# A bidirectional encoder layer on one core: the order of operand preparation in the down projection, and where the residual additions stand

## Chip, core and metric

One of the cores of a Trainium2 chip runs the whole program. The metric is the device time of one execution in microseconds; the kernel before takes 2554.81 us (median of 3 runs, 2551.83 to 2556.84). Less is better.

## What is computed

Two requests of 1024 tokens (with 16 meta tokens in front) go one after the other through the same layer in float32: attention and a gated linear recurrence side by side, an output projection, and a SwiGLU feed-forward block. The part at issue is the last:

```python
xn = rms_norm(h, norm_ffn_g[l])
g, u = jnp.split(xn @ w_gate_up[l], 2, axis=-1)   # 1024 -> 2 x 2816
h = h + (jax.nn.silu(g) * u) @ w_down[l]          # 2816 -> 1024, the down projection
...
h = rms_norm(h, final_norm_g)
```

## The kernel before

Each request is called a trunk. For each trunk the kernel runs a projection phase, attention, and `ffn`. A float32 product is made of three TensorE passes: each operand is split into a high part (a cast to the rounded type fp32r, on ACT) and a low part (the rest, a subtraction on DVE or POOL), and `mm3` adds high x high, high x low and low x high into one PSUM bank.

Both products of the feed-forward block are done with a seven-product (Strassen-like) scheme. The activations and the weight are cut into 2 x 2 blocks; sums and differences of blocks are multiplied, and each product is added into several blocks of the result. In the down projection the seven products are passes, `DN` = P1, P2, P4, P5, P7, P6, P3, in that order. A pass sums over 22 hidden tiles in `NC` = 11 **units** (index c). A unit is four `mm3`, one for each of four PSUM banks q: 12 matmuls of 128x128 by 128x512. Its operands are two tiles of the shape 2 x 512 (high and low): `sop`, made from an activation block `A[i, j, c]`, and `top`, made from rows of the down weight (`raws`, loaded to one of four buffers, or `trun`, rows kept through several passes).

What sets the order of work around the change:

- All engines run their own queue in order. The kernel writes the order itself: `ffn` goes through `units`, and at the start of unit n calls `prep(n)`, then issues the matmuls of unit n (`gu_unit` for gate and up, `dn_unit` for down).
- `prep(n)` prepares units ahead as long as operand tiles are left: `cap` = 6 of a ring of seven, a down unit takes two. So in a down pass, when unit n is issued, the operands of n and n+1 are under way and n+2 is prepared.
- `prep_dn(p, c)` is the first half: the sums and differences that the pass needs (in place, on blocks of activations or on weight rows), then the casts on ACT. P1 and P3 need no sums. P2 has one on DVE, P4 one on DVE and one that takes turns between DVE (even c) and POOL (odd c) as well as a copy on ACT, P5 two on DVE, P7 one on DVE, P6 one on DVE and two more of which one falls to DVE and one to POOL.
- `prep_dn_lo(p, c)` is the second half: the low part of `top` on DVE and that of `sop` on POOL. After it the raw buffer is free. `lows(m)` does this for all prepared units below m and then calls `load`, which issues on SP the load of the next raw tile into the buffer that came free; SP's queue waits there until the low part has read it.
- When a pass is done, its four banks are added into the residual `T.h` on DVE, one to four additions for each bank (`C[p]`). They are kept in the list `adds` and are issued within the units of the next pass, in `dn_unit`, after the matmuls of banks q = 1 and q = 3. All must be issued by the last unit, since the pass after that uses the same banks.

In the last pass of the first trunk (P3) the second trunk's inputs are loaded, normalised and transposed in between.

Of the kernel before, what the change touches and what calls it, by code (L numbers as in the profile page):

```python
# [36 lines left out]
NC = NHT // 2  # L37
# [207 lines left out]
def hymba_kernel(ctx, tc, ins, outs, dbg=None):  # L245
# [182 lines left out]
    def mm3(out, lh, ll, rh, rl, first, last, more=False):  # L428

        pe.matmul(out, lhsT=lh, rhs=rh, start=first, stop=False, skip_group_check=more)  # L430
        pe.matmul(out, lhsT=lh, rhs=rl, start=False, stop=False, skip_group_check=more)
        pe.matmul(out, lhsT=ll, rhs=rh, start=False, stop=last, skip_group_check=more)
# [1179 lines left out]
    def ffn_stream(T, b):  # L1612
# [42 lines left out]
        def load(limit=None):  # L1655

            while r_next[0] < len(items):
                i = r_next[0]
                if i >= 4 and items[i - 4][0] not in freed:
                    break  # L1660
                key, shape, parts = items[i]
                r = slot(raw_tags[i % 4], shape, name="wraw")
                for dst, src in parts:
                    sync.dma_start(out=dst(r), in_=src)
                raws[key] = r
                r_next[0] += 1
# [88 lines left out]
        def prep_dn_lo(p, c):  # L1755
            src, s, sop, top = half.pop((p, c))
            dve.tensor_tensor(top[:, 1], src, fv(top[:, 0]), ALU.subtract)
            pool.tensor_tensor(sop[:, 1], s, fv(sop[:, 0]), ALU.subtract)
            ops["dn", p, c] = (q4((sop[:, 0], sop[:, 1])), (top[:, 0], top[:, 1]))
            if p in ("P2", "P6", "P3"):  # L1760
                if c % 2 or c == NC - 1:
                    freed.add((p, c - c % 2))
            elif p in ("P4", "P5"):
                freed.add((p, c))
# [3 lines left out]
        def lows(n):  # L1768

            while n_lo[0] < min(n, T.n_prep2):  # L1770
                u = T.units[n_lo[0]]
                if u[0] == "dn":
                    prep_dn_lo(*u[1:])
                n_lo[0] += 1
            load()
# [3 lines left out]

        def prep(n):  # L1780

            lows(n + 2)
            while T.n_prep2 < len(T.units):
                u = T.units[T.n_prep2]
                need = 1 if u[0] == "gu" else 2
                out = sum(1 if x[0] == "gu" else 2 for x in T.units[n:T.n_prep2])
                if out + need > cap:
                    break
                if T.before_prep(u) is False:
                    break  # L1790
                (prep_gu if u[0] == "gu" else prep_dn)(*u[1:])
                T.n_prep2 += 1
                load()
            lows(n + 1)

        T.before_prep = lambda u: u[1:] == ("P1", 0)
        load()
        prep(0)
        T.prep_ops = prep

    def ffn(T, b, nxt):
# [9 lines left out]
        def bank(s, i, name):  # L1811
            tag = PB[s][i]
            return mk_d([P, 512], name) if tag is None else ps.tile([P, 512], F32, tag=tag, name=name)
# [113 lines left out]
        adds = []  # L1927
        banks = {}

        def add(p, q, i, l, sign, bk):  # L1930
            hs = T.h[:, 2 * q + i - 1, (l - 1) * 512:l * 512]
            dve.tensor_tensor(hs, hs, bk, ALU.add if sign > 0 else ALU.subtract)

        def dn_unit(p, c):
            n = DN.index(p)
            if c == 0:
                banks[n] = [bank(n % 2, q, "dn") for q in range(4)]
            (sh, sl), (th, tl) = ops.pop(("dn", p, c))
            for q in range(4):
                mm3(banks[n][q], sh[:, q], sl[:, q], th, tl, c == 0, c == NC - 1)  # L1940
                if q % 2 and adds:
                    adds.pop(0)()
            if c == NC - 1:
                assert not adds
                for q in range(4):
                    for i, l, sign in C[p]:
                        adds.append(lambda q=q, i=i, l=l, sign=sign, bk=banks[n][q]: (add(p, q, i, l, sign, bk), T.h_adds.add((p, q, i, l))))
# [103 lines left out]
        for n, (kind, p, i) in enumerate(units):  # L2051
            cur[0] = n
            if n == len(GU):
                for _ in side:
                    pass
            T.prep_ops(n)
            assert T.n_prep2 > n
            if kind == "gu":
                gu_unit(p, i)
                gu_hook(p, i)  # L2060
            else:
                dn_unit(p, i)
                if p == "P3" and not T.d_free and not adds:
                    T.d_free = True
                    if nxt is None:
                        gf_b = slot(S_GR, [P, D], name="gfin")
                        sync.dma_start(out=gf_b, in_=bcast_rows(ins["final_norm_g"]))
                        odd = spawn(finals(range(1, TT, 2), lambda t: True, slot("s4", [P, D], name="junk")), 3.0)
# [91 lines left out]
```

## Time and profile before

| | |
|---|---|
| median of 3 runs | 2554.81 us (2551.83 to 2556.84) |
| the profiled execution | 2563.52 us |
| its span, first to last instruction | 2561.7 us |
| mean granted TensorE clock | 0.97 |
| busy share PE / DVE / ACT / POOL | 93 / 70 / 46 / 52% |
| down projection, first trunk | 1021.95 to 1285.04 us |
| down projection, second trunk | 2298.05 to 2547.45 us |

Times in the rows are us from the span's start. PE is TensorE, with PEld its weight loads, which overlap the matmuls; DVE is VectorE, ACT ScalarE, POOL GpSimd, SP the queue that issues DMAs. `out<-in` are the program's names: `wop` an operand tile, `dn` the banks, `h` the residual, `wraw` and `trun` weight rows, and `aA`, `aB`, `aC`, `aD`, `aS`, `aV` the activation blocks. All compute instructions stand on line 118, that of a helper, so that groups are told apart by tiles.

### The profile page before, as it was taken

Reading aid. Unit: us, or ns where it says so; the run is one execution under the profiler, and the core shown is the slowest. Engines: PE = TensorE matmul, PEld = TensorE weight load, DVE = VectorE, ACT = ScalarE, POOL = GpSimd, SP = SyncE. Lnnn points to the kernel's source line nnn. Section 1 sums busy time; section 2 is a strip of 40 time slices with the busy share of each in tenths; the row PEclk is TensorE's granted clock in tenths of the full one; section 3 lists DMA queues with packets and bytes.
Section 4 is the critical chain, followed back from the end, with each engine's and each line's share of the span. In section 5 each row is a group of like instructions: output and inputs, shape, how many; then the busy total and the mean of one; then the engine's idle time right before and its main releaser. Section 6 shows DMA issues by size and latency. Waiting matters only on the chain.

```text
span 2561.7 us, 34088 instructions
## 1 busy us (share of the span) xinstructions
PE 2385.7 (93%) x12402; PEld 2002.5 (78%) x12402; DVE 1782.2 (70%) x2462; ACT 1168.3 (46%) x2083; POOL 1335.8 (52%) x1222
## 2 busy tenths in 40 slices
PE   7998999989999999998889889999799999999887
PEld 7878998867888888766677789988678888878665
DVE  6787888876555555778866778888665555557787
ACT  4456666654223232333535566666442222224434
POOL 5434766554444444445763356665544444444456
PEclk9998999989999999999999889999899999999999
DMA  5112000112222224741330130001122232247402
GB/s 137 37 35 101 19 17 18 42 66 65 76 78 82 88 74 156 271 148 38 136 128 19 35 108 18 9 18 42 66 66 74 83 91 74 83 159 276 149 30 111
DMA packets 189703, 212.77 MB, mean 83 GB/s; under 512 B 24272, under 2 KB 141008, under 8 KB 188512
## 3 DMA queue, kind: packets, MB, share of 16 engines
q1 hardware_dynamic: 189536, 210.60, 24.9%
q8 instruction: 98, 1.61, 0.3%
q14 instruction: 69, 0.57, 0.1%
HBM read 168.45 MB, written 39.85 MB: 81 GB/s over the span
## 4 chain that ended last, share of the span: by engine, by line
PE 65%; DVE 18%; ACT 6%; POOL 5%; issue 5%; DMA 1%; SPq 0%; ACTq 0%; DVEq 0%; POOLq 0%
PE gu L118 33%; PE op L118 5%; PE dn L118 5%; PE S L118 4%; PE pvo L118 4%; PE ptp L118 3%; DVE wop L118 3%; ACT wop L118 2%; PE pin L118 2%; PE qp L118 2%; DVE arena L118 2%; PE gp L118 2%; PE pg L118 1%; DVE m L118 1%; ACT arena L118 1%
## 5 line engine op out<-in xcount | busy, mean ns | idle before, releaser
L118 PE MATMUL dn<-wop 128*128 128x512 f32 x1848 | 463.4, 403 | 44.8 <-DVE wop L118 34.0
L118 PEld LDWEIGHTS dn<-wop 128*128 128x128 f32 x1848 | 340.7, 189 | 160.8 <-DVE wop L118 68.0
L118 PE MATMUL gu<-xT,wop 128*128 128x512 f32 x1408 | 371.2, 394 | 0.0
L118 POOL TENSOR_TENSOR pexp<-pexp,rsum 128x1024 f32<-128x1024 f32 x128 | 243.3, 1900 | 234.1 <-DVE rsum L118 150.7
L118 POOL TENSOR_TENSOR wop<-wraw,wop 128x512 fp32r<-128x512 f32 x176 | 230.7, 1311 | 217.0 <-ACT wop L118 217.0
L118 POOL TENSOR_TENSOR wop<-wsum,wop 128x512 fp32r<-128x512 f32 x132 | 171.7, 1301 | 269.0 <-ACT wop L118 269.0
L118 PEld LDWEIGHTS gu<-xT,wop 128*128 128x128 f32 x1408 | 264.0, 188 | 59.4
L118 PE MATMUL gu<-xB,wop 128*128 128x512 f32 x1056 | 265.5, 399 | 2.9 <-DVE xB L118 2.9
L118 ACT CAST wop<-wraw 128x512 fp32r<-128x512 f32 x264 | 162.5, 616 | 229.3 <-DVE wraw L118 159.9
L118 PE MATMUL gu<-xH,wop 128*128 128x512 f32 x1056 | 254.7, 396 | 1.7 <-DVE act L118 1.7
L118 PEld LDWEIGHTS gu<-xH,wop 128*128 128x128 f32 x1056 | 198.7, 188 | 50.5 <-issue 2.5
L118 PEld LDWEIGHTS gu<-xB,wop 128*128 128x128 f32 x1056 | 199.5, 190 | 49.0 <-DVE xB L118 3.6
L118 ACT CAST pt<-ptp 128x512 fp32r<-128x512 f32 x256 | 149.1, 586 | 127.9 <-PE ptp L118 126.7
L118 DVE TENSOR_REDUCE m<-S 128x1 f32<-128x1041 f32 x128 | 158.2, 1236 | 52.7 <-PE S L118 51.9
L118 ACT ACTIVATE pexp<-S,m 128x1041 f32<-128x1041 f32 x128 | 145.0, 1133 | 57.8 <-DVE m L118 55.1
L118 DVE TENSOR_TENSOR pt<-ptp,pt 128x512 fp32r<-128x512 f32 x256 | 168.2, 682 | 3.4 <-ACT pt L118 2.2
L118 PE MATMUL ptp<-idf,pexp 128*128 128x128 f32 x1024 | 157.0, 278 | 11.8 <-DVE pt L118 6.7
L118 PE MATMUL pvo<-pt,vst 128*128 128x256 f32 x1024 | 155.3, 295 | 3.6 <-DVE attnT L118 3.5
L118 PE MATMUL S<-kh,qs 128*128 128x348 f32 (+1 forms) x384 | 136.6, 358 | 19.3 <-ACT pexp L118 9.8
L118 ACT CAST wop<-wsum 128x512 fp32r<-128x512 f32 x132 | 81.8, 620 | 141.8 <-DVE wsum L118 141.8
L118 DVE SCALAR_TENSOR_TENSOR act<-th,act 128x512 f32<-128x512 f32 x88 | 143.8, 1634 | 3.0
L118 PEld LDWEIGHTS ptp<-idf,pexp 128*128 128x128 f32 x1024 | 126.9, 144 | 22.5 <-issue 7.8
(290 smaller groups left out, 5246.3 us busy)
## 6 DMA issues: line engine op xcount, KB each, us to landing
wraw<-in_w_gate_up SPq DMA_DIRECT2D x176, 256.0 KB, 3.5
wraw<-in_w_down SPq DMA_DIRECT2D x110, 256.0 KB, 2.8
ad<-act SPq DMA_DIRECT2D x44, 512.0 KB, 3.5
wraw<-in_w_down SPq DMA_DIRECT2D x22, 512.0 KB, 3.2
wraw<-in_w_in SPq DMA_DIRECT2D x32, 256.0 KB, 3.3
hd<-h SPq DMA_DIRECT2D x16, 512.0 KB, 5.1
h<-hd SPq DMA_DIRECT2D x16, 512.0 KB, 10.7
out<-h SPq DMA_DIRECT2D x15, 512.0 KB, 2.7
```

The lines of the kernel that those rows point to most:

```text
L118: return fn(*args, **kw)
```

## The change

Two edits. In `prep`, the low parts are no longer done at the start of the call: the loop with the sums and casts comes first (in a down pass, those of unit n+2), and then the low parts of all units up to n+1. In `dn_unit`, the additions of the pass before are no longer issued two in each unit until none is left. A unit now issues its share: the additions that are left, divided by the units that are left and rounded up (`due`), at most two; in P3, two a unit as before.

```diff
         def prep(n):
 
-            lows(n + 2)
             while T.n_prep2 < len(T.units):
...
                 (prep_gu if u[0] == "gu" else prep_dn)(*u[1:])
                 T.n_prep2 += 1
                 load()
-            lows(n + 1)
+            lows(n + 2)
...
             (sh, sl), (th, tl) = ops.pop(("dn", p, c))
+            due = -(-len(adds) // (NC - c)) if p != "P3" else min(2, len(adds))
             for q in range(4):
                 mm3(banks[n][q], sh[:, q], sl[:, q], th, tl, c == 0, c == NC - 1)
-                if q % 2 and adds:
+                if q % 2 and due:
+                    due -= 1
                     adds.pop(0)()
```

## Rows read from the trace of the kernel before

**Rows 1.** Page, groups: busy us, mean ns, then idle before and releaser.

```profile
L118 PE MATMUL dn<-wop 128*128 128x512 f32 x1848 | 463.4, 403 | 44.8 <-DVE wop L118 34.0
```

**Rows 2.** Windows by pass, P1 to P3 of trunk two; P4, P5, P7, P6, P3 of one.

```profile
core 0: us, PE busy (x) PEld busy (x) DVE busy (x) ACT busy (x) POOL busy (x), PEclk, DMA share, GB/s
2298.05:2331.46 33.41, 30.87 (x134) 24.74 (x132) 17.92 (x18) 13.53 (x24) 16.32 (x12) 1.00 0.89 339
2331.46:2362.05 30.59, 30.59 (x133) 24.81 (x132) 27.74 (x39) 12.66 (x23) 13.83 (x11) 1.00 0.54 204
2362.05:2400.21 38.16, 34.18 (x133) 24.20 (x132) 26.93 (x31) 16.62 (x30) 20.79 (x15) 1.00 0.39 138
2400.21:2436.33 36.12, 33.58 (x133) 23.97 (x132) 28.30 (x37) 13.58 (x22) 14.21 (x11) 1.00 0.46 160
2436.33:2472.52 36.19, 33.61 (x133) 23.97 (x132) 27.58 (x32) 12.66 (x22) 15.07 (x13) 1.00 0.00 1
2472.52:2516.68 44.16, 34.74 (x134) 23.94 (x133) 41.18 (x42) 15.04 (x25) 37.81 (x23) 1.00 0.19 66
2516.68:2547.45 30.77, 30.77 (x133) 24.63 (x131) 19.68 (x24) 15.29 (x35) 18.48 (x21) 1.00 0.21 76
...
1087.42:1125.63 38.21, 34.17 (x133) 24.18 (x132) 26.98 (x31) 16.64 (x30) 20.87 (x15) 1.00 0.40 138
1125.63:1161.74 36.11, 33.50 (x133) 23.95 (x132) 28.29 (x37) 13.57 (x22) 14.23 (x11) 1.00 0.45 160
1161.74:1198.21 36.47, 33.58 (x134) 23.95 (x132) 27.85 (x32) 12.66 (x22) 15.05 (x13) 1.00 0.01 2
1198.21:1242.32 44.11, 34.61 (x134) 23.95 (x132) 41.19 (x42) 14.57 (x24) 37.77 (x23) 1.00 0.21 72
1242.32:1285.04 42.72, 39.98 (x197) 30.43 (x195) 36.16 (x44) 26.89 (x50) 25.67 (x26) 1.00 0.41 148
```

**Rows 3.** Timeline, P7 of trunk two: start, us, instruction, then idle before and releaser.

```profile
2443.43 0.68 DVE L118 TENSOR_TENSOR aD<-aA,aD 128x512 f32<-128x512 f32 x1
...
2444.20 0.62 ACT L118 CAST wop<-aD 128x512 fp32r<-128x512 f32 x1 [2.15 <-DVE aD L118]
...
2444.95 1.30 POOL L118 TENSOR_TENSOR wop<-aD,wop 128x512 fp32r<-128x512 f32 x1 [1.99 <-ACT wop L118]
2445.38 1.42 DVE L118 TENSOR_TENSOR wop<-trun,wop 128x512 fp32r<-128x512 f32 x1
2446.72 0.68 DVE L118 TENSOR_TENSOR aD<-aA,aD 128x512 f32<-128x512 f32 x1
```

**Rows 4.** Timeline, P6 of trunk two, DVE and POOL.

```profile
2488.31 1.80 POOL L118 TENSOR_TENSOR wop<-aA,wop 128x512 fp32r<-128x512 f32 x1
2488.90 1.75 DVE L118 TENSOR_TENSOR aA<-aC,aA 128x512 f32<-128x512 f32 x1
...
2490.07 1.74 POOL L118 TENSOR_TENSOR trun<-trun,wraw 128x512 f32<-128x512 f32 x1
...
2490.69 1.67 DVE L118 TENSOR_TENSOR aS<-aS,aA 128x512 f32<-128x512 f32 x1
...
2491.76 1.75 POOL L118 TENSOR_TENSOR wop<-aA,wop 128x512 fp32r<-128x512 f32 x1
...
2494.08 0.68 DVE L118 TENSOR_TENSOR aA<-aC,aA 128x512 f32<-128x512 f32 x1
...
2494.68 0.68 DVE L118 TENSOR_TENSOR trun<-trun,wraw 128x512 f32<-128x512 f32 x1
```

**Rows 5.** Windows, instructions on `dn` alone: P4's last eight units, P6's first and second four.

```profile
core 0: us, PE busy (x) PEld busy (x) DVE busy (x), PEclk, DMA share, GB/s
...
2370.40:2400.21 29.81, 25.83 (x97) 17.43 (x96) 0.00 (x0) 1.00 0.40 141
2472.52:2488.69 16.17, 12.63 (x49) 8.70 (x48) 3.82 (x6) 1.00 0.14 49
2488.69:2504.85 16.16, 12.62 (x49) 8.71 (x48) 1.27 (x2) 1.00 0.18 66
```

**Rows 6.** Page, DMA issues: count, KB each, median us to landing.

```profile
wraw<-in_w_down SPq DMA_DIRECT2D x110, 256.0 KB, 2.8
```

**Rows 7.** Groups in P3 of trunk one, PE: the next trunk's transposes.

```profile
L118 PE MATMUL tp<-idf,xn 128*128 128x128 f32 x64 | 9.8, 275 | 0.6 <-DVE xn L118 0.4 <-DVE xsXL L118 0.3
```

## The prediction

> **What bounds the kernel now.** I read the groups of the page first, then the windows by pass, then the timeline inside one pass. In the groups the reader is to see that the matmuls of the down projection are the only large matmul group that stands idle for another engine: 44.8 us, of which 34.0 us ended with a low part made on DVE [rows 1]. That number is a floor, since a matmul that has begun and waits for its weights counts as busy. So I went by passes: each pass is 11 units of 12 matmuls, and the windows give its length [rows 2]. In the second trunk P2 and P3 take 30.59 and 30.77 us, about 2.79 us per unit, while P4 takes 38.16, P5 36.12, P7 36.19 and P6 44.16. The granted clock is 1.00 in all of them, so these passes do the same TensorE work at the same clock and the rest is waiting. Against 30.7 us each, the four slow passes lose 7.5 + 5.4 + 5.5 + 13.5 = 31.9 us per trunk; the first trunk's are within 0.3 us of them. That is all that there is to win. P1 (33.41) has no sums, so nothing of it is reordered; P3 of the first trunk (42.72) has 64 transposes for the next trunk in it [rows 7] and no sums either.
>
> **Why a slow pass is slow.** P7 shows it plainly [rows 3]. DVE takes a difference of activations (aD) at 2443.43. ACT's cast of it starts at 2444.20, after 2.15 us without work that this difference ended. POOL's low part starts at 2444.95 and ends at 2446.25. DVE's own low part is issued at 2445.38 and takes 1.42 us, where such an operation takes 0.68 with POOL at rest [rows 4]: it ends 0.55 us after POOL does. Only then, at 2446.72, comes the next unit's difference. So one round is sum, cast, POOL's low part, DVE's low part: 3.29 us, which is the pass (36.19 / 11). It is a circle made by the order of DVE's queue: the low part, which waits for ACT and POOL, stands ahead of the next sum, which waits for nothing.
>
> **DVE and POOL also hold each other up**, and this decides how much can be had. In P6 POOL's instructions end at 2490.11, 2491.81 and 2493.51, and between them DVE's two-input sums end 0.54 to 0.55 us after POOL does [rows 4]: strictly in turns, 1.70 us for one of each. Two DVE sums with no POOL in between are 0.60 us apart (2494.08, 2494.68) [rows 4]. A P6 unit has three such DVE operations and two of POOL, or, over two units, four pairs and two singles: 4 x 1.70 + 2 x 0.60 = 8.0 us. Measured are 16.17 and 16.16 us for four units [rows 5], 8.08 for two. So P6 is already at what this taking of turns allows, and no order of its queue makes it shorter.
>
> **The change, part by part.** *Order.* Sums and casts of unit n+2 now stand on DVE, ACT and POOL ahead of the low parts of unit n+1. Nothing is added or removed: no instruction, no DMA. The circle opens: while ACT casts n+2, DVE makes the low part of n+1, whose casts are one unit old. What is late next is either TensorE (2.79 us per unit) or the turns of DVE and POOL, counted from the code:
> - P7: two DVE, one POOL: 1.70 + 0.60 = 2.30 us, under 2.79. The pass falls to 30.7: gain 5.5 and (36.47) 5.8, together 11.3 us.
> - P5: three DVE, one POOL: 1.70 + 1.20 = 2.90, over 2.79. 11 x 2.90 = 31.9 against 36.1: 4.2 a trunk, 8.4.
> - P4: even and odd units together five DVE, three POOL: 5.10 + 1.20 = 6.30, or 3.15 a unit. Its last eight units now take 29.81 [rows 5], 3.73 each; 11 of these would be 41.0, so the pass starts with 2.8 us of work done ahead during P2. After: 11 x 3.15 - 2.8 = 31.9 against 38.2: 6.3 a trunk, 12.7 with roundings.
> - P6: no gain of its own, but P7 will now run ahead of TensorE by 2.79 - 2.30 = 0.49 a unit, and so hand it the same 2.8 us that P2 hands P4: 5.6 for both trunks.
>
> The sum is 38.0 us. Two of P6's units took 8.08 where the turns give 8.00, one per cent, and P4 and P5 have more places where both engines wait for ACT; I take off 2 us for that: **36 us**.
>
> For the turns I weigh a rule. By the trace one DVE and one POOL operation take 1.70 us in turns, less than the 0.68 + 1.30 that they take alone [rows 3, 4]. The Trainium skill (SBUF — State Buffer, Who interferes with whom) says that a DVE instruction with two SBUF inputs and a GpSimd instruction that reads SBUF exclude each other for the whole instruction. Taken at the recorded lengths, that gives P6 4.64 us a unit, and the trace, at 4.04, does not agree; the exclusion is there, its length is shorter.
>
> *The same sum with whole lengths*, as the dear end: P5 3 x 0.68 + 1.30 = 3.34 a unit, no gain; P4 (3.40 + 3.90) / 2 = 3.65, 0.9 a trunk; P7 2.66, still under TensorE, 11.3; with P6's 5.6 it is 18.7 us. The cheap end, no taking of turns in P4 and P5: 15.0 + 10.8 + 11.3 + 5.6 = 42.7. I take 1.70 because P6 confirms it over eight units.
>
> *Additions.* They go from two a unit until done to one, or two where 16 are due; the same number in all. They read PSUM and one SBUF tile, and in P6 they cost nothing: four units with six of them took 16.17 us, four with two 16.16 [rows 5]. P2, with two a unit, runs at full rate [rows 2]. So 0; the cover is POOL's holding of its turn. If it were gone, P6 alone has no room on DVE (41.18 of 44.16 us busy, [rows 2]): four moved additions of 0.68, 2.7 us a trunk either way. The banks that they free are wanted one pass later; only P2's reach into the last unit, and those are for the bank that the next pass comes to in the last quarter of its first unit.
>
> *Loads.* A raw tile's reload waits on SP for the low part that read it, and that part now stands behind one unit's sums, at most three turns, 5.1 us. A load takes about 2.8 us [rows 6] and four tiles give it three units, some 8.4 us: together under the time, with 0.5 us to spare at the worst, so 0; where it failed, the sums of P4 would wait by the excess alone. SP has nothing else behind those loads but the next of them.
>
> The profiled execution is 2563.5 us, 8.7 above the median; the sum is of differences, so 2563.5 - 36 = 2527.5 there, and from the median 2554.8 - 36 = **2519 us**.
>
> **The rivals.** (a) *The turns are dear*: P4 and P5 stay and only P7 and what it hands to P6 are won, 18.7 us: 2536. For it, the recorded lengths and DVE's strict order, which can leave both engines waiting for ACT; against it, eight units of P6 at 8.08. (b) *The turns bind less than they seem*: P4 and P5 at TensorE's rate, 2512; if even P6 followed, at 13.5 a trunk in place of 2.8, 2491. For it, nothing but that reordering might pair the engines better; against it, rows 4. (c) *The order is not what holds the casts*: they would wait for a free operand tile (seven in the ring, two a unit) and nothing moves: 2555. Against it, the cast's wait ended with DVE's difference [rows 3], and P2 runs at full rate with the same ring. (d) *Slower: the low part comes late.* TensorE needs the low part of n+1 at the second matmul, and it now stands behind the sums of n+2 on DVE and POOL. It decides from the point at which DVE is not a unit ahead; then every unit of P4, P5 and P6 waits for one more DVE turn, 0.55 us: 66 units, 36 us, less P7's 11.3, about 25: 2580. Against it, the queue is a round: what comes later in one unit has been done earlier in the one before, and a shift is paid once a pass, not once a unit.
>
> **How the numbers follow.** Forecast 0.70, (a) 0.12, (b) 0.08, (c) 0.05, (d) 0.05. A measurement of this kernel tells about 0.2%, 5 us, from no change. Forecast, (a) and (b) are faster: 0.90; (c) is the same: 0.05; (d) slower: 0.05. The range goes from the cheap end for P4 and P5 with the unknown of the additions on top (42.7 + 2.7, some 45: 2510, and 2 more for the spread of the runs, 2508) to (a) with the like (2537). It leaves out (c), (d) and most of (b)'s lower half.
>
> **What would show it.** Right: P7 at 30.7 us, with DVE's next difference starting before the last unit's low part; P5 near 32, P4 near 32; P6 near 41, its first three units at 2.8 and the rest at 4.0; P2 and P3 unchanged. P5 at 36 would be (a) or (c), told apart by P7. P6 under 38 would be (b). Wrong altogether: P7 unchanged, or low parts waited for by TensorE in P2, which now never waits.

## The result, and the profile after

The changed kernel takes 2519.18 us (median of 4 runs, 2517.27 to 2520.11) against 2555.82 (2551.83 to 2558.39) in the same comparison: the ratio is 0.9857, with a 95% interval of 0.9840 to 0.9874. That is 36.6 us faster; 36 were forecast.

The windows by pass of the changed kernel, P4, P5, P7 and P6 of the second trunk, then P6 and P3 of the first (columns as in [rows 2]):

```profile
2333.81:2366.77 32.96, 31.46 (x133) 24.59 (x132) 32.82 (x33) 16.74 (x30) 23.79 (x15) 1.00 0.48 160
2366.77:2398.41 31.64, 31.64 (x134) 24.13 (x132) 31.58 (x37) 13.66 (x23) 17.73 (x12) 1.00 0.56 183
2398.41:2429.05 30.64, 30.64 (x133) 24.82 (x132) 30.61 (x32) 12.77 (x22) 17.46 (x13) 1.00 0.03 8
2429.05:2473.02 43.97, 34.51 (x133) 24.05 (x132) 42.70 (x40) 13.90 (x23) 35.65 (x22) 1.00 0.18 62
1182.52:1226.56 44.04, 34.47 (x133) 24.03 (x132) 42.25 (x40) 13.43 (x22) 35.13 (x21) 1.00 0.29 94
1226.56:1266.58 40.02, 39.09 (x197) 30.52 (x195) 36.28 (x45) 27.29 (x50) 24.90 (x25) 1.00 0.37 129
```

Against [rows 2], P4 went from 38.16 to 32.96, P5 from 36.12 to 31.64 and P7 from 36.19 to 30.64, TensorE's own rate. In P5 and P7 TensorE's busy time is now the whole pass (P5 still loses 1 us against the 30.6 of P2, inside its matmuls, since one that waits for its weights counts as busy). P6 did not move (44.16 to 43.97), though it was to get 2.8 us. The first trunk's P3 fell by 2.7 us, which was not forecast. DVE's busy share has risen in the faster passes (P7: 27.58 of 36.19 before, 30.61 of 30.64 now): much of that is time in which it stands in turn behind POOL, and it costs the pass nothing while TensorE has its operands.

The circle of [rows 3] is open. The timeline of P7 after the change, DVE with the ACT cast and POOL's low part between (start, us, instruction, idle before and releaser):

```profile
2404.54 0.68 DVE L118 TENSOR_TENSOR wop<-trun,wop 128x512 fp32r<-128x512 f32 x1
...
2405.14 0.67 DVE L118 TENSOR_TENSOR h<-h,dn 128x512 f32<-128x512 f32 x1
...
2405.45 1.30 POOL L118 TENSOR_TENSOR wop<-aD,wop 128x512 fp32r<-128x512 f32 x1 [1.39 <-ACT wop L118]
2405.74 1.56 DVE L118 TENSOR_TENSOR aD<-aA,aD 128x512 f32<-128x512 f32 x1
2407.22 0.68 DVE L118 TENSOR_TENSOR wop<-trun,wop 128x512 fp32r<-128x512 f32 x1
```

Before, the low part (`wop<-trun`) took 1.42 us behind POOL and the next difference (`aD`) had to wait for it. Now the difference stands behind POOL's operation (1.56 us), the low part follows at once without waiting for ACT, and the round is 2.68 us, under the 2.79 that TensorE takes.

Where the time came from: by windows, the down projection went from 263.1 + 249.4 to 244.8 + 234.0 us, that is 33.7 less. The median fell by 36.6. The two profiled executions differ by more, 43.4 us, and the rest of that lies in the second trunk's projection and attention. Their windows before (first two lines) and after:

```profile
1285.04:1499.90 214.86, 187.58 (x996) 160.84 (x996) 148.82 (x187) 109.64 (x191) 102.17 (x108) 0.92 0.19 60
1499.90:1860.00 360.10, 330.62 (x2254) 303.82 (x2254) 288.87 (x485) 227.09 (x416) 221.15 (x231) 0.94 0.12 43
```

```profile
1266.58:1477.90 211.32, 183.58 (x997) 157.24 (x996) 148.60 (x187) 108.86 (x191) 104.13 (x108) 0.95 0.20 61
1477.90:1831.80 353.90, 326.07 (x2254) 300.17 (x2254) 287.48 (x485) 227.16 (x416) 223.66 (x231) 0.96 0.13 44
```

The granted clock stood at 0.92 and 0.94 there before and at 0.95 and 0.96 after. From the end of the first down projection to the start of the second, the kernel before took 1013.0 us, two others with the old order 1009.0 and 1003.7 (experiments 2 and 8 below), and the seven kernels with the new order 1001.3 to 1005.7. So an old order can be as fast there, and I don't count these 9.7 us as the change's. The 2.9 us by which the median fell more than the passes I can't place.

### The profile page after: what moved, and what is told of

Same layout as the page of the kernel before. It is cut to its first block, busy times and chain, and to the rows that moved or that the text cites. A ratio compares the mean times of both kernels' runs of the same rounds, so it can differ in the third digit from the quotient of the medians.

```text
span 2518.1 us, 34092 instructions
## 1 busy us (share of the span) xinstructions
PE 2358.0 (94%) x12402; PEld 1996.2 (79%) x12402; DVE 1809.5 (72%) x2462; ACT 1168.2 (46%) x2083; POOL 1354.6 (54%) x1222
## 4 chain that ended last, share of the span: by engine, by line
PE 67%; DVE 21%; ACT 4%; issue 3%; POOL 3%; DMA 0%; SPq 0%; DVEq 0%; POOLq 0%; ACTq 0%
PE gu L118 34%; PE dn L118 6%; PE op L118 5%; PE S L118 4%; PE pvo L118 4%; PE ptp L118 3%; DVE wop L118 3%; PE qp L118 3%; PE pin L118 2%; DVE arena L118 2%; PE pg L118 2%; DVE h L118 2%; DVE wraw L118 1%; PE gp L118 1%; DVE m L118 1%
## 5 line engine op out<-in xcount | busy, mean ns | idle before, releaser
L118 PE MATMUL dn<-wop 128*128 128x512 f32 x1848 | 446.7, 399 | 27.5 <-DVE wop L118 18.1
L118 PE MATMUL S<-kh,qs 128*128 128x348 f32 (+1 forms) x384 | 135.7, 356 | 20.6 <-ACT pexp L118 11.3
```

Source lines behind the costliest of these rows:

```text
L118: return fn(*args, **kw)
```

## The experiments

Eight kernels, each timed beside the kernel before (2556 to 2557 us in these comparisons).

**1. The order alone.** The changed kernel with the additions as before:

```diff
-            due = -(-len(adds) // (NC - c)) if p != "P3" else min(2, len(adds))
...
-                if q % 2 and due:
-                    due -= 1
+                if q % 2 and adds:
                     adds.pop(0)()
```

> The changed kernel with the additions issued as before (two a unit until done). Theory (the order opens the circle, DVE and POOL take turns): the whole gain stays, 2519 us within 4; P7 30.6 us, P5 31.6, P4 33.0 as in the changed kernel. Rival (the spread of the additions is what keeps DVE ahead): P7, where eight additions then fall into four units, or P2 goes back up by 2 us or more a trunk, 2525 or over. For P6, which took 44.0 us with units of 4.29 where 4.04 was expected: if the additions are what costs (an addition stands on DVE while POOL waits for the next difference, 0.6 us in two units), the units after the first five, which have none, take 4.04; if the new order itself pairs the engines worse, they stay at 4.29.

Measured: 2525.22 us (ratio 0.9877, 0.9862 to 0.9892), 6 us slower than the change. P7 and P4 kept their gain (30.65 and 32.47 in the second trunk), but P5 went to 36.80 and, in the first trunk, 37.69. So the rival had it right that the spread matters, with the pass wrong: it is P5. Windows of P5, of P6, of three late units of P6, and of the one bad unit of P5:

```profile
2369.47:2406.27 36.80, 32.94 (x133) 25.61 (x132) 29.33 (x41) 13.87 (x24) 25.74 (x13) 0.95 0.49 157
2436.92:2479.27 42.35, 34.66 (x134) 25.38 (x132) 41.10 (x37) 13.26 (x22) 34.44 (x22) 0.96 0.17 56
2464.86:2476.47 11.61, 9.27 (x37) 6.52 (x36) 11.36 (x9) 4.15 (x7) 10.38 (x7) 1.00 0.27 91
...
2381.09:2389.21 8.12, 4.26 (x13) 3.02 (x12) 4.99 (x7) 1.65 (x3) 8.12 (x4) 0.84 0.63 198
```

One unit takes 8.12 us (in the first trunk 8.94). The timeline shows what it waits for, POOL, DVE and TensorE:

```profile
2378.02 7.51 POOL L118 TENSOR_TENSOR wop<-aC,wop 128x512 fp32r<-128x512 f32 x1 [1.49 <-ACT wop L118]
...
2378.31 0.68 DVE L118 TENSOR_TENSOR aC<-aD,aC 128x512 f32<-128x512 f32 x1
...
2378.91 0.68 DVE L118 TENSOR_TENSOR wraw<-wraw 128x512 f32<-128x512 f32 x1
...
2383.72 0.68 DVE L118 TENSOR_TENSOR aB<-aB 128x512 f32<-128x512 f32 x1
2384.35 1.72 DVE L118 TENSOR_TENSOR wraw<-wraw 128x512 f32<-128x512 f32 x1
...
2385.58 4.62 PE L118 MATMUL dn<-wop 128*128 128x512 f32 x12 [3.86 <-POOL wop L118]
```

POOL's low part is issued at 2378.02 and ends 7.51 us later. In between DVE makes ten two-input operations 0.60 us apart (2378.31 to 2383.72), each at its full speed. POOL is not served in turn here: it is done only when the eleventh operation has been issued (2384.35, 0.63 us behind the tenth and itself held up to 1.72 us). What let it in then, the rows don't show. TensorE waits 3.86 us for that low part, and afterwards its granted clock is at the lower of its two levels, 1.2 GHz, for a while (0.84 of full over this stretch), so the unit grows by more than the wait. In the changed kernel the four additions of this pass stand one in each of four units; an addition reads PSUM, and POOL's operation runs beside it (one at 2372.51 took its usual 0.68 us inside POOL's 2372.23 to 2373.74). That this is how the spread helps is not shown: the units of that P5 without an addition take turns with POOL too. Shown is that P5 has the long unit with the additions as before and not when they are spread. In P6 three units behind the additions took 11.61 us, 3.87 each, so the new order by itself does not cost 4.29 there; the expectation on that point, 4.04, held roughly.

**2. The additions alone.** The kernel before with `due`, and the old order in `prep`:

> The kernel before with the additions spread as in the change, and the old order. Theory: nothing to gain, 2556 us within 4; P7 stays at 36.2, P5 36.1, P4 38.2, P6 44.1. Rival (the additions stood in the circle): P7, where they are spread most, gets shorter by 0.6 us for each unit that loses one, 2 us or more a trunk, 2551 or less.

Measured: 2557.36 us (ratio 1.0004, 0.9994 to 1.0013): nothing. P5 and P7 of the second trunk stand where they were in [rows 2]:

```profile
2392.62:2428.76 36.14, 33.57 (x134) 23.94 (x132) 29.07 (x37) 13.58 (x22) 14.25 (x11) 1.00 0.49 160
2428.76:2465.19 36.43, 33.67 (x133) 23.94 (x132) 27.53 (x32) 12.66 (x22) 15.00 (x13) 1.00 0.01 2
```

With the circle closed, DVE pauses in every unit of P5 (0.22 us where there is an addition, 0.82 where there is none), and POOL's low part takes its 1.30 us; the spread has nothing to do. It is worth 6 us only with the new order.

**3. P6's additions in another place.** The changed kernel; in P6 each addition stands behind the unit's first difference:

```diff
                 dve.tensor_tensor(A[1, 1, c], A[2, 2, c], A[1, 1, c], ALU.subtract)
+                if c > 2 and T.adds:
+                    T.adds.pop(0)()
...
-            due = -(-len(adds) // (NC - c)) if p != "P3" else min(2, len(adds))
+            due = 0 if p == "P6" else -(-len(adds) // (NC - c)) if p != "P3" else min(2, len(adds))
```

> The changed kernel; in P6 the eight additions are issued on DVE right behind the unit's first difference, which POOL waits for, and not behind the low part. Theory (in P6 an addition was exposed in every second unit, since POOL waited behind it): units of 4.0 to 4.1 us, P6 41.6 us a trunk in place of 44.0, 2514 us. Rival (the new order costs P6 0.25 us a unit by itself): P6 stays at 44, 2519.

Measured: 2518.8 us (ratio 0.9851, 0.9836 to 0.9866), not told from the change by the whole time. P6 fell by 1.3 us a trunk, half of what was expected. The windows of P6 in the second trunk and of six of its units:

```profile
2429.21:2471.88 42.67, 33.39 (x134) 24.01 (x133) 42.49 (x40) 13.59 (x23) 34.94 (x22) 1.00 0.19 63
2440.21:2465.05 24.84, 18.47 (x74) 13.06 (x72) 24.84 (x25) 7.34 (x13) 19.34 (x13) 1.00 0.19 64
```

The units take 4.14 us. In the changed kernel four units on `dn` alone took 17.18, 4.30 each, and its timeline shows where an addition is exposed (DVE, and POOL's sum that waits):

```profile
2440.05:2457.23 17.18, 12.77 (x49) 8.72 (x48) 2.70 (x4) 1.00 0.18 62
```

```profile
2445.86 0.68 DVE L118 TENSOR_TENSOR h<-h,dn 128x512 f32<-128x512 f32 x1
2446.46 0.68 DVE L118 TENSOR_TENSOR aA<-aC,aA 128x512 f32<-128x512 f32 x1
...
2447.22 1.68 POOL L118 TENSOR_TENSOR aS<-aS,aA 128x512 f32<-128x512 f32 x1 [1.83 <-DVE aA L118]
```

The addition at 2445.86 runs while POOL has nothing (1.83 us idle, ended by the difference that stands behind the addition): in every second unit 0.6 us that nothing hides, 0.30 a unit. Experiment 5 below has units of P6 in the new order with no addition: they take 3.99 us, and POOL's idle time there is 1.23. So the growth of P6's units (4.30 against 4.04 before) goes with the additions and not with the order alone. The place tried here gets 0.16 us a unit back; why not all of it, I did not settle.

**4. POOL's low part twice in P7.**

```diff
             pool.tensor_tensor(sop[:, 1], s, fv(sop[:, 0]), ALU.subtract)
+            if p == "P7":
+                pool.tensor_tensor(sop[:, 1], s, fv(sop[:, 0]), ALU.subtract)
```

> The changed kernel; in P7 POOL makes the low part of the activation operand twice (the same values). Theory (DVE and POOL exclude each other, 1.70 us for one of each): a P7 unit has two of each, 3.40 us, over TensorE's 2.79: P7 rises from 30.6 to about 37 less the 2 to 3 us done ahead, so 35 to 37, and P6, which then gets nothing handed over, rises by up to 2.8: 2519 + 2 x 7, 2530 to 2537 us. Rival (they run side by side and POOL's own time alone counts): 2 x 1.30 = 2.60 us a unit, under TensorE's, P7 stays at 30.6 and the kernel at 2519.

Measured: 2538.76 us (ratio 0.9927, 0.9910 to 0.9943), just above the expected range. The windows of nine units of P7 in the second trunk, of the pass, and of its last unit:

```profile
2411.54:2442.14 30.60, 27.56 (x110) 19.57 (x108) 30.60 (x27) 10.39 (x18) 29.35 (x19) 1.00 0.00 1
2408.75:2449.12 40.37, 34.99 (x133) 24.97 (x132) 40.34 (x33) 12.77 (x22) 38.54 (x24) 0.96 0.03 8
2442.14:2449.12 6.98, 4.64 (x13) 3.19 (x12) 6.95 (x5) 1.24 (x2) 6.48 (x4) 0.76 0.14 38
```

Nine units in 30.60 us are 3.40 each, two pairs of 1.70 to the hundredth, with POOL busy 29.35 of them. The rival's 2.60 would have left the pass at 30.6. The pass is 3 us longer than expected because its last unit took 6.98: it waits 2.30 us for its own low part, which POOL makes twice and behind P6's first sum, and again the granted clock drops to the lower level with the wait (0.76). P6, which was to rise by up to 2.8 us, took 43.20.

**5. The spread in P5 alone.** The changed kernel with one addition a unit in P5 and two a unit elsewhere:

```diff
-            due = -(-len(adds) // (NC - c)) if p != "P3" else min(2, len(adds))
+            due = -(-len(adds) // (NC - c)) if p == "P5" else min(2, len(adds))
```

> The changed kernel with the additions spread (one a unit) in P5 alone, and two a unit in every other pass. With two a unit everywhere, P5 took 37.7 and 36.8 us, since one low part on POOL took 7.5 us while DVE made ten two-input operations 0.60 us apart; P6 took 42.3, less than the 44.0 of the changed kernel. Theory (an addition, which reads PSUM, is the gap in which POOL gets its turn, and P5 is the pass that needs such gaps): P5 31.6, P6 42.3, 2525 - 11 = 2514 us. Rival (POOL's loss of its turn comes from elsewhere, the raw loads or chance): P5 stays near 37, 2525.

Measured: 2514.44 us (ratio 0.9844, 0.9827 to 0.9860), as the theory had it; one of the four runs took 2519.09, so the gain of 5 us over the change is read from the passes more than from the whole time. P5 and P6 of the second trunk:

```profile
2362.08:2393.71 31.63, 31.63 (x133) 24.11 (x132) 31.57 (x37) 13.67 (x23) 17.72 (x12) 1.00 0.56 183
2424.36:2467.10 42.74, 34.82 (x134) 25.28 (x132) 41.48 (x38) 13.39 (x23) 34.83 (x22) 0.96 0.16 56
```

P5 is whole again. So P5 is the pass that needs the spread, and in P6 the spread costs about 1.2 us a trunk. P6 shows the price of an addition, too. The windows of one of its units with two additions and of four behind the additions, and POOL's sum in one of these four:

```profile
2434.00:2440.50 6.50, 4.81 (x14) 3.26 (x12) 6.46 (x6) 1.54 (x3) 5.44 (x4) 0.75 0.22 80
2448.33:2464.30 15.97, 12.44 (x50) 8.71 (x49) 15.70 (x12) 5.39 (x9) 13.51 (x9) 1.00 0.29 99
```

```profile
2450.47 1.68 POOL L118 TENSOR_TENSOR aV<-aV,aB 128x512 f32<-128x512 f32 x1 [1.23 <-DVE aB L118]
```

Without an addition the units take 3.99 us, what the turns of the prediction give (4.00). With two additions in a unit, single units are long, the one above at the lower clock for part of it; spread, each of eight units pays 0.30. Over the pass the first comes out cheaper.

**6. All of it on DVE.** The changed kernel; in P4, P5 and P6 DVE makes every sum and both low parts:

```diff
-            turn = (dve, pool)[c % 2]
+            turn = dve
...
-                (pool, dve)[c % 2].tensor_tensor(A[1, 2, c], A[1, 2, c], A[1, 1, c], ALU.subtract)
+                dve.tensor_tensor(A[1, 2, c], A[1, 2, c], A[1, 1, c], ALU.subtract)
...
-            pool.tensor_tensor(sop[:, 1], s, fv(sop[:, 0]), ALU.subtract)
+            (dve if p in ("P4", "P5", "P6") else pool).tensor_tensor(sop[:, 1], s, fv(sop[:, 0]), ALU.subtract)
```

> The changed kernel; in P4, P5 and P6 all sums and both low parts are made on DVE, and POOL does none. Theory (one in turn with POOL costs 1.70 us, two on DVE alone 1.20): P4 and P5 four operations, 2.4 us a unit, both at TensorE's 30.7; P6 five and an addition in eight of eleven units, 3.0 to 3.6 us, 11 x 3.4 - 2.8 = 35 in place of 44.0: per trunk 2.3 + 0.9 + 9, 2519 - 24 = 2495 us. Rival (DVE is the bound by its own recorded time, 0.68 an operation, and its waits): P6 5 x 0.68 + 0.5 = 3.9 a unit, 40 us or more, P4 and P5 unchanged or worse: 2511 or more.

Measured: 2493.4 us (ratio 0.9753, 0.9738 to 0.9767), 26 us less than the change and the fastest of all with the next one. P4, P5, P7 and P6 of the second trunk, and DVE's timeline in P6:

```profile
2321.56:2352.18 30.62, 30.62 (x133) 24.80 (x132) 30.07 (x50) 17.26 (x31) 0.00 (x0) 1.00 0.57 191
2352.18:2382.74 30.56, 30.56 (x133) 24.81 (x132) 27.89 (x44) 13.07 (x22) 4.58 (x3) 1.00 0.50 171
2382.74:2413.39 30.65, 30.65 (x133) 24.80 (x132) 28.08 (x38) 12.57 (x22) 10.97 (x9) 1.00 0.05 18
2413.39:2447.48 34.09, 32.96 (x133) 24.40 (x132) 32.53 (x53) 13.27 (x22) 5.69 (x3) 1.00 0.20 70
```

```profile
2427.70 0.68 DVE L118 TENSOR_TENSOR h<-h,dn 128x512 f32<-128x512 f32 x1
2428.30 0.68 DVE L118 TENSOR_TENSOR aA<-aC,aA 128x512 f32<-128x512 f32 x1
...
2431.31 0.68 DVE L118 TENSOR_TENSOR h<-h,dn 128x512 f32<-128x512 f32 x1
```

P4 and P5 run at TensorE's rate and P6 falls from 43.97 to 34.09. From one addition to the next are 3.61 us: six operations 0.60 apart, five of the unit and the addition. The engine that was given all the work binds less, since an operation of POOL cost DVE 1.10 us of waiting (1.70 less its own 0.60) and costs 0.60 when DVE does it.

**7. All on DVE, additions two a unit.** The kernel of 6 with the additions of 1:

> As the kernel with all of P4, P5 and P6 on DVE, with the additions two a unit until done. Theory (the spread matters only where POOL must find a gap): with POOL out of these passes the spread does nothing: the same time as with it, within 4 us, and P5 without its long unit, 30.7. Rival (early additions put DVE itself behind): P5 keeps a unit of 8 us, slower by 6 or more.

Measured: 2493.23 us (ratio 0.9754, 0.9739 to 0.9768), the same as 6; P5 is 30.56 and P6 34.08 in the second trunk. The spread matters only where POOL has to get in.

**8. All on DVE in the old order.** The kernel before with the edit of 6:

> The kernel before (low parts first, additions two a unit) with all sums and low parts of P4, P5 and P6 on DVE. Theory (two costs that are separate: the circle through ACT, and the turns with POOL): the circle stays; P7, where POOL remains, 36.3; P5 sum 1.2, two casts behind it to the second's end 0.85, both low parts 1.2: 3.25 a unit, 36 as before; P4 the same 3.25, 33 to 34 in place of 38.2; P6 3.3 in place of 4.0, 36 to 37: 2556 - 24 = 2532 us. Rival (POOL's turns are all there is): P5 and P4 at 30.7, 2520 or less.

Measured: 2541.7 us (ratio 0.9943, 0.9928 to 0.9958). P4, P5, P7 and P6 of the second trunk:

```profile
2348.77:2382.57 33.80, 33.27 (x133) 24.32 (x132) 27.33 (x44) 15.70 (x28) 0.00 (x0) 1.00 0.45 156
2382.57:2419.62 37.05, 35.56 (x133) 23.91 (x132) 29.24 (x48) 13.56 (x22) 1.03 (x1) 1.00 0.46 156
2419.62:2455.96 36.34, 33.60 (x134) 23.96 (x133) 28.33 (x34) 12.66 (x22) 13.23 (x11) 1.00 0.00 1
2455.96:2495.38 39.42, 35.29 (x133) 23.92 (x132) 38.45 (x61) 15.04 (x25) 3.16 (x2) 1.00 0.21 74
```

As expected, the circle stays with no POOL in it (P5 37.05, P4 33.80), and P7, where POOL remains, takes 36.34. The kernel won 14 us where 24 were expected. P6 took 39.42 in place of 36 to 37 (four units with additions took 4.2 us each, the later ones 3.3), and the first trunk's P3 46.19 in place of 42.72, which I had left out. There are two costs, since each edit wins by itself, but they don't simply add up: with the additions as before, taking POOL out brings 14 us in the old order and 32 in the new one (1 against 7), and the order brings 31 with POOL (1) and 48 without (7 against 8).

## Why the prediction was right, point by point

- **The circle** (sum, cast, POOL's low part, DVE's low part) was the bound of P5 and P7, and the new order opens it. P7 gained 5.9 + 5.6 = 11.4 us where 11.3 were forecast. Experiments 2 and 8 show it from the other side: in the old order P5 and P7 stay at 36 to 37, whatever is done to the additions, and P5 even with POOL out of it.
- **The turns of DVE and POOL**, 1.70 us for one of each, decide what comes next. P5 was forecast at 2.90 us a unit, 31.9 in all, and took 31.64: 9.0 for both trunks against 8.4. Experiment 4 measured the price by itself: 3.40 for two pairs. The dear end of the sum, whole recorded lengths (P5 at 3.34, no gain), is out.
- **P4**: forecast 31.9, measured 32.96 and 33.00, 10.4 us won against 12.7. The unit was right: in the second trunk six units from 2344.96 to 2363.97 took 19.01 us, 3.17 each against 3.15. The term that was mis-sized is the work done ahead: 11 x 3.17 - 32.96 leaves 1.9 us, not the 2.8 of [rows 5]. About 0.5 of that is the spread: with the additions two a unit P4 took 32.47 and 32.51 (experiment 1).
- **P6** is the step that failed: "no gain of its own, but P7 will now run ahead ... and so hand it the same 2.8 us". Both halves of it left out the additions. P7's round, counted as 2.30 us, is 2.68 with an addition in it, so P7 gains 0.11 us a unit on TensorE and not 0.49, and hands over less. P6's first two units (on `dn` alone) took 6.85 us after the change, and 5.54 in experiment 5, where P7's additions are not spread (in this order):

```profile
2429.05:2435.90 6.85, 6.22 (x25) 4.36 (x24) 0.67 (x1) 1.00 0.13 49
...
2424.36:2429.90 5.54, 5.54 (x26) 4.51 (x24) 1.27 (x2) 1.00 0.00 1
```

  And P6's own units went from 4.04 to 4.30. Eleven of these would be 47.3 us; it took 43.97, so 3.3 us of work was done ahead, and the longer units ate it. That no order makes P6's units shorter held (3.99 without additions); I had not asked whether an addition in each makes them longer.
- **Additions: "So 0"** was wrong in both directions, and the errors covered each other. In P6 one addition a unit costs 0.3 us a unit (experiments 3 and 5); against two a unit, the spread costs 1.2 us a trunk there and 0.5 in P4. In P5 the spread keeps POOL from being passed over, and is worth 5 to 6 us a trunk (experiments 1 and 5). The cover that I had named, POOL holding its turn, is there only where POOL has something to do at that moment.
- **Loads**: as forecast. Among the waits of the changed kernel in P4 to P6 of either trunk there is none of an engine for a load.
- **The first trunk's P3**, forecast unchanged, gave 2.7 us. In P3 ACT squares the next trunk's rows, in its queue among the casts. Before, its first square waited for the load; after, it did not. ACT's and SP's timelines, before and then after:

```profile
1246.68 1.06 ACT L118 ACTIVATE junk<-xn 128x1024 f32<-128x1024 f32 x1 [2.96 <-DMA xn<-in_x_sample]
...
1238.39 4.39 SPq L95 DMA_DIRECT2D xn<-in_x_sample  x6
```

```profile
1227.86 1.05 ACT L118 ACTIVATE junk<-xn 128x1024 f32<-128x1024 f32 x1
...
1219.83 4.43 SPq L95 DMA_DIRECT2D xn<-in_x_sample  x6
```

  P3 begins at 1242.32 before and at 1226.56 after. The six loads are thus issued 3.9 us ahead of it before and 6.7 us after, as the preparation now runs ahead of TensorE. That the wait of 2.96 us is the cause of the 2.7 is read from these rows; no run separates it. It does go with the order: the seven kernels with the new order had 40.0 to 40.6 us in this pass, the three with the old one 42.1 to 46.2.
- The sum, then: 11.4 + 9.0 + 10.4 + 0.3 + 2.7 = 33.8 in the passes, against 36 forecast. The agreement of the median to a fraction of a microsecond has some luck in it: P6 and P4 brought 7.6 us less than their terms of 5.6 and 12.7, and P3's 2.7, P5's extra 0.6, the 2 us taken off and some 2.8 us outside these passes made up for it.
- Of the rivals, (a) needed P5 at 36 and (c) P7 at 36: neither came. (b) needed P6 under 38, which came only when POOL was taken out. (d) needed P4 and P5 to grow, and they fell by 5.2 and 4.5 us a trunk; what made P6's units longer was the additions.

## What to carry to other kernels

Where an engine's queue holds a step that waits for another engine ahead of a step that waits for nothing, put the free step first: here that alone broke a round of 3.29 us, and no engine did less. Where two engines take turns, count their operations together (here 1.70 us for one of each), and where one is slower, giving its work to the other can win (26 us here) though it makes the busier one busier. And an operation that costs nothing where it stands can cost or save something where it is moved to: here the additions did both. Ask what the other engine does at that moment.

## What the runs showed that was not expected

- A POOL operation that waits for its turn can be passed over again and again: ten DVE operations of two SBUF inputs, 0.60 us apart, went ahead of one that had been issued before the first of them, and it took 7.51 us in place of 1.30 (experiment 1). In P6 and P7 the two took strict turns, and in the changed kernel's P5 they did so even in units without an addition. What decides between the two I did not settle. The Trainium skill (SBUF — State Buffer, Who interferes with whom) says that whoever issues first gets the shared ports and the other waits until the first is finished; this case agrees for single pairs (in P7 after the change DVE's difference ends 0.55 us behind POOL's low part), but not for a row of DVE operations, where the first to wait was not the next to be served.
- Giving both engines' work to one nearly halves the loss against TensorE's 2.79: P6 went from 4.30 to 3.61 us a unit with five operations and an addition on DVE alone.
- With waits of TensorE came a granted clock at the lower level: with one of 3.86 us in experiment 1 (0.84 over the stretch), with one of 2.30 in experiment 4 (0.76), and with two of 1.06 and 0.63 in the unit of 6.50 us in experiment 5 (0.75). So a unit that waits 3.86 us took 8.12 where 2.79 is normal, 5.3 more.
